# A y step's exp(cum) computed on ScalarE from the row tile already loaded, with that row loaded three slots ahead

## The chip, the cores and the metric

One core of a Trainium2 chip runs the whole kernel as one launch. The metric is the device time of that launch in microseconds (us), median over runs. Engines are named as the profile names them: PE is TensorE's matmuls, PEld its weight loads, DVE is VectorE, ACT is ScalarE, POOL is GpSimd, SP is SyncE, which issues most of the DMAs. POOL issues DMAs too, in its own instruction order.

## What is computed

The reference is one layer of a hybrid sequence mixer: an adaLN-modulated input, one input projection, two branches (a gated linear recurrence A and a Mamba-2 style scan B, both in two directions), gates, and an output projection with a layer norm. The change lies in branch B. Cut to what matters:

```python
cum = jnp.cumsum((dt * a_neg)..., axis=2)            # within a chunk of 128 tokens
y_inter = jnp.einsum('bktgn,bktgr,bkgrnp->bktgrp', cc, jnp.exp(cum), s_prev)
cb = jnp.einsum('bktgn,bksgn->bktsg', cc, bc)
lmat = masked_exp(cum[:, :, :, None] - cum[:, :, None, :], causal)
y_intra = jnp.einsum('bktsg,bktsgr,bksgrp->bktgrp', cb, lmat, x_dt)
return (y_inter + y_intra)
```

There are 1024 latent tokens (8 chunks of 128), 16 heads of 64 channels in 4 groups, a state of 128, and two directions. So `exp(cum)` of a chunk is a row per head and direction, wanted on all 128 partitions.

## The kernel before

All projections are three-pass fp32r matmuls in 128-column blocks (`mm3`, lines 178 to 180). Branch A comes first (to about 560 us of the profile), then branch B in four windows, one for each head group g (`b_window`), then the output projections.

`b_scan(g)` (lines 796 to 912) is the hand-written order of a group: masks and transposes, nine state positions (`xw` on POOL at L843, two matmuls into `bu` at L846, two DVE additions into `St`), then the y loop. The y loop has 16 steps (2 head pairs j, 8 chunks t), each handled in four stages that lag behind one another by `LAGS` slots:

- `loads`: POOL issues a DMA that spreads the row `cum` of two heads and two directions (512 numbers) over 128 partitions, tile L, from the DRAM copy `cum_d` (L868).
- `exponents`: POOL issues a second such DMA, tile e, from `ecum_d`, which holds exp(cum) (L868 again); DVE takes the minimum of L with the tokens' own cum (L878); ACT takes four exps of 128x128 in place, each with its bias column (L881).
- `products`: POOL multiplies e by C (L886), DVE multiplies L by the masked C·B (L887).
- `y_matmuls`: PE multiplies x by L and the states by e into the PSUM tile yi (L902); after four chunks DVE adds yi to y (L905).

Tiles L and e come from a pool of 12 buffers (`w2`) that the state stage and the rms stage share. `cum_d` and `ecum_d` are written once, early, by SP (L703), eight copies of each.

Between the yields of `b_scan` a filler puts projection work of the next group and gates onto PE (`Fill.window`): each yield carries a weight (`W_SCAN` 0.45 for a state position, `W_Y` 0.43 for a y slot) times the group's rate `FILL_B`; a unit is 24 matmuls of 512 columns. Their results go through ACT and DVE too (convolution at L746 and L749, SiLU at L761, gates at L611, weight splits at L162 and L163). A scheduler then sets the order within each engine from the code's order and priorities; each engine runs its own order strictly.

Of the kernel before, what the change touches and what calls it, by code (L numbers as in the profile page):

```python
# [8 lines left out]
P = 128  # L9
# [21 lines left out]
GRAIN = 512  # L31
FILL_T, FILL_A = 0.8, 0.8
GA = (2, 0, 0, 6)
FILL_B = (0.74, 0.64, 0.64, 0.8)
OUT1, OUT2 = 8, 3
GATES = (2, 1, 1, 4)
W_0, W_PRE, W_SCAN, W_Y = 2.0, 1.0, 0.45, 0.43
LAGS = (0, 1, 2, 4)
REP = 8
DT_MIN = 2.0 ** -60  # L40
QT = P
NQT = L // QT
# [61 lines left out]
def hybrid(tc, x, c, ctx, c_ctx, w_mod, b_mod, w_in, lb_logits, a_norm_w, conv_w, conv_b, dt_bias,  # L104
# [3 lines left out]
    nc = tc.nc  # L108
    V, S, T, G = nc.vector, nc.scalar, nc.tensor, nc.gpsimd
# [5 lines left out]
    def pool(st, name, bufs=1, **kw):  # L115
        return st.enter_context(tc.tile_pool(name=name, bufs=bufs, **kw))

    with root:
# [3 lines left out]
        dp = pool(root, "dram", space=DRAM)  # L122
# [5 lines left out]
        def sc(name):  # L128
            return ps.tile([P, 512], F32, tag="sc", bufs=5, name=name)
# [25 lines left out]
        gb_d = dp.tile([D, L], F32, name="gb_d")  # L155

        cum_d = dp.tile([REP, NQT, BH, 2, QT], F32, name="cum_d")
        ecum_d = dp.tile([REP, NQT, BH, 2, QT], F32, name="ecum_d")


        def split(raw, hi, lo):
# [64 lines left out]
        WU = tp_.tile([P, 2, NTA, BH], F32, name="WU")  # L226
        DEC = tp_.tile([P, 2, NTA, BH], F32, name="DEC")
# [5 lines left out]
        with ExitStack() as st:  # L233
# [9 lines left out]
            rows = sp.tile([P, P], F32, name="rows")  # L243
# [186 lines left out]
        def gt(tag, bufs, shape, name):  # L430
            return gp.tile([P] + list(shape), F32, tag=tag, bufs=bufs, name=name)
# [184 lines left out]
        def time_steps():  # L616
# [29 lines left out]
            for i in range(NTA):  # L646
                dst = ta[:, i * 64:(i + 1) * 64] if i < NT else tb[:, (i - NT) * 64:(i - NT + 1) * 64]
# [41 lines left out]
            V.tensor_tensor(fl(WU), fl(WU), DTf, ALU.mult)  # L689
            yield 1.0  # L690

            rows_ = gt("S", 1, [2, L], "crow")[:2 * BH]
            crow, erow = rows_[:, 0, :], rows_[:, 1, :]
            for b in range(2):
                tr = sc(f"cr{b}")
                for i in range(4):
                    T.transpose(tr[:2 * BH, i * P:(i + 1) * P],
                                CUr[:, (b * 4 + i) * 2 * BH:(b * 4 + i + 1) * 2 * BH], ident)
                S.copy(crow[:, b * 512:(b + 1) * 512], tr[:2 * BH, :])
                S.activation(erow[:, b * 512:(b + 1) * 512], tr[:2 * BH, :], AF.Exp)  # L700
            for r_ in range(REP):
                for src, dst in ((crow, cum_d), (erow, ecum_d)):
                    nc.sync.dma_start(dst[r_].rearrange("q h d t -> (h d) q t"),  # L703
                                      src.rearrange("h (q t) -> h q t", t=QT))

        fill = Fill()
        ua = [{} for _ in range(AH)]
# [86 lines left out]
        orders = ((8, 9, 0, 1, 2, 3, 4, 5, 6, 7), (9, 8, 7, 6, 5, 4, 3, 2, 1, 0))  # L794

        def b_scan(g, u):
# [5 lines left out]
            for i0, n in ((8, 2), (0, 4), (4, 4)):  # L802
                tx = sc(f"bb{g}_{i0}")
                for i in range(n):
                    src = Bc[:, (i0 + i) * P:(i0 + i + 1) * P] if i0 < NT else u["Bc"][:, i * P:(i + 1) * P]
                    T.transpose(tx[:, i * P:(i + 1) * P], src, ident)
                S.copy(bt[i0 // 4] if i0 < NT else btc, tx[:, :n * P].rearrange("p (a b) -> p a b", a=n))
            b_tok = lambda i: bt[i // 4][:, i % 4, :] if i < NT else btc[:, i - NT, :]

            CB = bt_("CB", 1, [2, L], f"CB{g}")  # L810
            for b in range(2):
                cb = sc(f"cb{g}_{b}")
                for i in range(4):
                    t = (b * 4 + i) * P
# [6 lines left out]
            xt = bt_("xt", 1, [NT, 2 * P], f"xt{g}")  # L821
            xtc = w2([NTC, 2 * P], f"xtc{g}")
            for i0 in (8, 0, 6, 2, 4):
                tx = sc(f"bx{g}_{i0}")
                for i in range(2):
                    for j in range(2):
                        src = xc[:, j, (i0 + i) * P:(i0 + i + 1) * P] if i0 < NT else u["xcc"][:, j, i * P:(i + 1) * P]
# [1 line left out]
                S.copy(xt[:, i0:i0 + 2, :] if i0 < NT else xtc, tx[:].rearrange("p (a b) -> p a b", a=2))  # L829
            yield W_PRE  # L830

            St = bt_("St", 1, [NT, 2, 256], f"St{g}")
            prev = None
            for pos in range(NTA - 1):
                i0, i1 = orders[0][pos], orders[1][pos]
                by_h = lambda t_: sub(t_[:], i0 * BH + HPG * g, [[(NTA + i1 - i0) * BH, 2], [1, HPG], [0, 64]])
                if pos < NTC:
                    xs_ = sub(xtc[:], (i0 - NT) * 256, [[(i1 - i0) * 256, 2], [64, HPG], [1, 64]])
                else:
                    xs_ = sub(xt[:], i0 * 256, [[(i1 - i0) * 256, 2], [64, HPG], [1, 64]])  # L840
                xw = w2([2, 256], f"xw{g}_{pos}")
                xw4 = xw[:].rearrange("p d (a b) -> p d a b", b=64)
                G.tensor_tensor(xw4, xs_, by_h(WU), ALU.mult)  # L843
                ub = sc(f"bu{g}_{pos}")
                for d, i in ((0, i0), (1, i1)):
                    T.matmul(ub[:, d * 256:(d + 1) * 256], b_tok(i), xw[:, d, :], start=True, stop=True)  # L846
                ub3 = ub[:].rearrange("p (d b) -> p d b", d=2)
                if pos == 0:
                    s0 = w2([2, 256], f"s0{g}")
                    prev = s0[:]  # L850
                    S.copy(prev, ub3)
                else:
                    cur = St[:, pos - 1]
                    V.tensor_tensor(cur.rearrange("p d (a b) -> p d a b", b=64),
                                    prev.rearrange("p d (a b) -> p d a b", b=64), by_h(DEC), ALU.mult)
                    V.tensor_tensor(cur, cur, ub3, ALU.add)
                    prev = cur
                yield W_SCAN


            y = xc
            steps = [(j, t) for j in range(2) for t in range(NT)]
            Ls, Cs, yis = {}, {}, {}

            def rows(src_d, name, j, t):
                t_ = w2([2, 2, P], f"{name}{g}_{j}_{t}")
                src = src_d[0, t, HPG * g + 2 * j, 0, 0:1]
                G.dma_start(t_[:].rearrange("p a b c -> p (a b c)"),  # L868
                                  bass.AP(src.tensor, src.offset, [[NQT * BH * 2 * QT, REP], [0, P // REP], [1, 4 * QT]]))
                return t_  # L870

            def loads(j, t):
                Ls[j, t] = rows(cum_d, "L", j, t)

            def exponents(j, t):
                Cs[j, t] = rows(ecum_d, "e", j, t)
                Lm, h0 = Ls[j, t], HPG * g + 2 * j
                V.tensor_tensor(Lm, Lm, sub(CU[:], t * BH + h0, [[1, 2], [NT * BH, 2], [0, P]]), ALU.min)  # L878
                for h in range(2):
                    for d in range(2):  # L880
                        S.activation(Lm[:, h, d, :], Lm[:, h, d, :], AF.Exp, bias=BIA[:, d, t, h0 + h:h0 + h + 1])  # L881
# [22 lines left out]
                    bs = slice((t - 3) * P, (t + 1) * P)  # L904
                    V.scalar_tensor_tensor(y[:, j, bs], xc[:, j, bs], bd_col(2 * g + j), yi, ALU.mult, ALU.add)  # L905

            for k in range(len(steps) + LAGS[-1]):
                for lag, stage in zip(LAGS, (loads, exponents, products, y_matmuls)):
                    if 0 <= k - lag < len(steps):
                        stage(*steps[k - lag])  # L910
                yield W_Y
# [4 lines left out]
        def z_proj(g, u):  # L916
            for j in range(2):
                blk = 2 * g + j
                for t0, n, acc in (proj_k if blk == 2 * BG - 1 else proj)(O_Z + blk * P, parts_l, f"z{blk}"):
                    if acc is None:  # L920
                        yield n / GRAIN / 4
                        continue
                    with ahead():
                        zs = bt_("gb", 4, [512], f"z{blk}_{t0}")
                        S.activation(zs, acc, AF.Silu)  # L925
                    if g + 1 < BG:
                        z_mul(u, j, t0, zs)
                    else:
                        z_last.append((u, j, t0, zs))
                    yield n / GRAIN / 4  # L930
# [58 lines left out]
        for g in range(BG):  # L989
# [9 lines left out]
            else:  # L999
                fill.add(z_proj(g, ub_[g]), f"z{g}")  # L1000
            fill.window(b_window(g), FILL_B[g])
            fill.until(f"b{g + 1}")
        g = BG - 1
# [129 lines left out]
```

## Time and profile before

| | us |
|---|---|
| median of 3 runs | 1306.72 (1305.6 to 1309.83) |
| the profiled execution | 1304.58 |
| its span | 1302.8 |
| PE busy | 1241.5 (95%) |
| DVE busy | 752.9 (58%) |
| ACT busy | 533.9 (41%) |
| POOL busy | 236.8 (18%) |

Busy shares are means over stages of different kinds. PE's ends are modelled, so a busy PE is not always a PE at its peak. Rows of a group name a line, an engine, the output and inputs, the count, busy time and mean, and then the idle time of that engine just before, with what ended it. The y loops lie at about 583 to 657, 728 to 797, 863 to 933 and 986 to 1062 us.

### The profile page before, as it was taken

What the parts mean: (1) busy time and instruction counts of PE and PEld (TensorE: products, weight loads), DVE (VectorE), ACT (ScalarE), POOL (GpSimd) and SP (SyncE); (2) the same over time, 40 slices, a digit from 0 to 9 for tenths busy, and PEclk for the clock granted to TensorE, in tenths of its full rate; (3) what the DMA queues carried; (4) which work ended last, traced back from release to release, by engine and by line L of the source; (5) the groups of instructions that cost most, each with busy time, mean ns of one, the idle gap of its engine ahead of it and who ended that gap; (6) DMA issues with size and microseconds to landing.
All of it is one profiled execution on the core that took longest, in us unless ns stands there. A gap on an engine that the chain in (4) does not pass through costs nothing.

```text
span 1302.8 us, 18836 instructions
## 1 busy us (share of the span) xinstructions
PE 1241.5 (95%) x7624; PEld 1004.4 (77%) x7624; DVE 752.9 (58%) x988; ACT 533.9 (41%) x851; POOL 236.8 (18%) x264
## 2 busy tenths in 40 slices
PE   5999999999999999999899979998899989999997
PEld 2778888888888888887688757876687668888886
DVE  2426745733836624667575577657646445575568
ACT  2436343432343333337442745364638453213110
POOL 1220000000000000044610662156226520000000
PEclk8999999999999999999999989999899989999999
DMA  9511312112112223125611663156416635662412
GB/s 317 182 40 49 82 33 92 42 35 65 33 33 70 71 75 97 33 65 151 152 39 49 156 147 71 33 147 162 136 58 164 171 98 193 225 248 95 156 41 97
DMA packets 126838, 137.02 MB, mean 105 GB/s; under 512 B 15568, under 2 KB 102288, under 8 KB 126752
## 3 DMA queue, kind: packets, MB, share of 16 engines
q1 hardware_dynamic: 107744, 102.09, 24.8%
q0 software_dynamic: 18656, 33.69, 10.8%
q8 instruction: 60, 0.98, 0.3%
q14 instruction: 26, 0.21, 0.1%
q10 hardware_dynamic: 352, 0.05, 0.0%
HBM read 115.55 MB, written 20.19 MB: 104 GB/s over the span
## 4 chain that ended last, share of the span: by engine, by line
PE 69%; issue 14%; POOL 7%; DVE 4%; DMA 3%; ACT 2%; SPq 0%; POOLq 0%; DVEq 0%; ACTq 0%
PE x L178 4%; PE x L179 3%; PE x L180 3%; POOL e L886 3%; PE f L180 3%; PE f L178 3%; PE f L179 2%; PE ga L178 2%; PE pl L520 2%; PE fo L179 2%; PE fo L180 2%; PE fo L178 2%; PE ga L180 2%; PE ga L179 2%; PE pb L178 2%
## 5 line engine op out<-in xcount | busy, mean ns | idle before, releaser
L881 ACT ACTIVATE L<-L,BIA 128x128 f32<-128x128 f32 x256 | 81.6, 391 | 88.0 <-DVE L L878 87.7
L886 POOL TENSOR_TENSOR e<-e,C 128x512 f32<-128x512 f32 x64 | 92.7, 1448 | 107.5 <-DMA e<-ecum_d 100.6
L843 POOL TENSOR_TENSOR xw<-xtc,WU 128x512 f32<-128x512 f32 x8 | 8.2, 1043 | 566.0 <-ACT xtc L829 566.0
L878 DVE TENSOR_TENSOR L<-L,CU 128x512 f32<-128x512 f32 x64 | 51.1, 800 | 70.4 <-DMA L<-cum_d 51.7
L902 PE MATMUL yi<-L,xt 128*64 128x128 f32 x512 | 44.3, 296 | 28.5 <-DVE L L887 21.8
L887 DVE TENSOR_TENSOR L<-L,CB 128x512 f32<-128x512 f32 x64 | 66.3, 1051 | 6.0 <-ACT L L881 5.9
L902 PEld LDWEIGHTS yi<-L,xt 128*64 128x64 f32 x512 | 28.2, 142 | 51.6 <-DVE L L887 28.3
L749 DVE SCALAR_TENSOR_TENSOR xc<-x,par,xc 128x496 f32<-128x496 f32 (+1 forms) x64 | 47.1, 735 | 13.8 <-ACT xc L746 12.7
L512 ACT COPY KX<-K 128x1024 f32<-128x1024 f32 x28 | 32.1, 1145 | 50.2 <-DVE K L531 45.1
L562 DVE SCALAR_TENSOR_TENSOR S<-S,T,ub 128x128 f32<-128x128 f32 x64 | 22.3, 348 | 51.3 <-ACT S L558 27.6
L178 PE MATMUL fo<-wo,mh 128*128 128x512 f32 x128 | 50.2, 392 | 0.0
L180 PE MATMUL fo<-wo,mh 128*128 128x512 f32 x128 | 49.8, 389 | 0.0
L179 PE MATMUL fo<-wo,ml 128*128 128x512 f32 x128 | 49.8, 389 | 0.0
L531 DVE TENSOR_TENSOR K<-K,T 128x1280 f32<-128x1280 f32 x28 | 46.4, 1658 | 3.4 <-ACT KX L512 1.6
L902 PE MATMUL yi<-e,St 128*64 128x128 f32 x512 | 41.7, 286 | 2.9 <-POOL e L886 2.9
L868 POOL DMA_DIRECT2D L<-cum_d x64 | 39.7, 620 | 0.8 <-DVE L L878 0.7
L533 DVE TENSOR_TENSOR Q<-Q,T 128x1024 f32<-128x1024 f32 x28 | 37.7, 1346 | 3.0 <-PE pl L520 3.0
L868 POOL DMA_DIRECT2D e<-ecum_d x64 | 39.1, 611 | 0.5 <-PE gb L180 0.5
L936 DVE TENSOR_TENSOR xc<-xc,z 128x512 f32<-128x512 f32 x16 | 11.6, 723 | 47.5 <-ACT z L925 47.5
L520 PEld LDWEIGHTS pl<-Q,KX 128*64 128x64 f32 x896 | 30.1, 138 | 9.4 <-issue 8.3
L902 PEld LDWEIGHTS yi<-e,St 128*64 128x64 f32 x512 | 32.3, 145 | 3.8 <-POOL e L886 3.6
L520 PE MATMUL pl<-Q,KX 128*64 128x64 f32 x896 | 34.1, 230 | 0.7 <-DVE Q L533 0.7
(996 smaller groups left out, 3738.9 us busy)
## 6 DMA issues: line engine op xcount, KB each, us to landing
L<-cum_d POOLq DMA_DIRECT2D x64, 256.0 KB, 5.2
e<-ecum_d POOLq DMA_DIRECT2D x64, 256.0 KB, 5.1
wm<-in_w_mod_dram SPq DMA_DIRECT2D x16, 512.0 KB, 7.9
xt<-in_x_dram SPq DMA_DIRECT2D x8, 512.0 KB, 8.4
ga_d<-ga SPq DMA_DIRECT2D x16, 256.0 KB, 2.0
gb_d<-gb SPq DMA_DIRECT2D x16, 256.0 KB, 2.4
m<-ga_d SPq DMA_DIRECT2D x8, 512.0 KB, 4.4
gbt<-gb_d SPq DMA_DIRECT2D x8, 512.0 KB, 7.2
```

Of the source, the lines that this page charges most:

```text
L178: T.matmul(dst, ah, bh, start=(first and i == 0), stop=False)
L179: T.matmul(dst, al, bh, start=False, stop=False)
L180: T.matmul(dst, ah, bl, start=False, stop=(last and i == n - 1))
L520: T.matmul(pl[rows_, t * HP:(t + 1) * HP], KX[:, o:o + HP], qx, start=True, stop=True)
L531: V.tensor_tensor(kv, kv, sub(Ta, lv, [[w, NA // w], [NA - lv, 2], [0, lv]]), ALU.mult)
L749: V.scalar_tensor_tensor(d3[:, :, a:z], r3[:, :, a + o:z + o], cw_col(t, blk), d3[:, :, a:z], ALU.mult, ALU.add)
L868: G.dma_start(t_[:].rearrange("p a b c -> p (a b c)"), bass.AP(src.tensor, src.offset, [[NQT * BH * 2 * QT, REP], [0, P // REP], [1, 4 * Q ...
L878: V.tensor_tensor(Lm, Lm, sub(CU[:], t * BH + h0, [[1, 2], [NT * BH, 2], [0, P]]), ALU.min)
L881: S.activation(Lm[:, h, d, :], Lm[:, h, d, :], AF.Exp, bias=BIA[:, d, t, h0 + h:h0 + h + 1])
L886: G.tensor_tensor(C4, C4, Cc[:, ts].unsqueeze(1).broadcast_to([P, 4, P]), ALU.mult)
L887: V.tensor_tensor(Lm, Lm, CB[:, :, ts].unsqueeze(1).broadcast_to([P, 2, 2, P]), ALU.mult)
L902: T.matmul(yi[h * 64:(h + 1) * 64, o], a, r, start=(k == 0), stop=(k == 3))
```

## The change

exp(cum) of a step is no longer loaded: ACT computes it from tile L (a 128x512 exp into e) before DVE's minimum overwrites L. `ecum_d`, its eight stores and its 64 loads are gone. `LAGS` becomes (0, 3, 4, 5): L is loaded three slots before its exponents, products come one slot after those, the matmuls one slot after the products. The first three loads are issued at state positions 3, 5 and 7 (`EARLY`), so the y loop starts at slot 3 and has 18 slots instead of 20. `FILL_B` is raised. The helper functions of the y loop are moved above the state loop, unchanged but for what is shown.

```diff
-FILL_B = (0.74, 0.64, 0.64, 0.8)
+FILL_B = (0.79, 0.68, 0.68, 0.85)
-LAGS = (0, 1, 2, 4)
+LAGS = (0, 3, 4, 5)
+EARLY = (3, 5, 7)
...
-        ecum_d = dp.tile([REP, NQT, BH, 2, QT], F32, name="ecum_d")
...
-                S.activation(erow[:, b * 512:(b + 1) * 512], tr[:2 * BH, :], AF.Exp)
             for r_ in range(REP):
-                for src, dst in ((crow, cum_d), (erow, ecum_d)):
-                    nc.sync.dma_start(dst[r_].rearrange("q h d t -> (h d) q t"),
-                                      src.rearrange("h (q t) -> h q t", t=QT))
+                nc.sync.dma_start(cum_d[r_].rearrange("q h d t -> (h d) q t"),
+                                  crow.rearrange("h (q t) -> h q t", t=QT))
...
             def exponents(j, t):
-                Cs[j, t] = rows(ecum_d, "e", j, t)
                 Lm, h0 = Ls[j, t], HPG * g + 2 * j
+                Cs[j, t] = w2([2, 2, P], f"e{g}_{j}_{t}")
+                S.activation(Cs[j, t], Lm, AF.Exp)
                 V.tensor_tensor(Lm, Lm, sub(CU[:], t * BH + h0, [[1, 2], [NT * BH, 2], [0, P]]), ALU.min)
...
                     prev = cur
+                if pos in EARLY:
+                    loads(*steps[EARLY.index(pos)])
                 yield W_SCAN
...
-            for k in range(len(steps) + LAGS[-1]):
+            for k in range(len(EARLY), len(steps) + LAGS[-1]):
```

What the scheduler makes of it is shown at two places, both in group 1 at the start of its y loop. In the changed kernel the loads are line 837, the new exp 847, the minimum 848, the four exps 851, the product on POOL 856, on DVE 857, and the y matmuls 872. A name such as L_0_3_5895 is tile L of head pair 0, chunk 3.

POOL in the kernel before, from the last state position on:

```order
L843 TENSOR_TENSOR xw_8_5832<-xt_5454,WU 128x512
L868 DMA L_0_0_5845<-cum_d 128x1x512
L868 DMA L_0_1_5853<-cum_d 128x1x512
L868 DMA e_0_0_5855<-ecum_d 128x1x512
L868 DMA L_0_2_5871<-cum_d 128x1x512
L868 DMA e_0_1_5873<-ecum_d 128x1x512
L868 DMA L_0_3_5895<-cum_d 128x1x512
L886 TENSOR_TENSOR e_0_0_5855<-e_0_0_5855,C_4625 128x512
L868 DMA e_0_2_5897<-ecum_d 128x1x512
L886 TENSOR_TENSOR e_0_1_5873<-e_0_1_5873,C_4625 128x512
```

Here each product stands behind its own load of e and the loads of the next steps.

POOL in the changed kernel at the same place:

```order
L837 DMA L_0_2_5812<-cum_d 128x1x512
L889 TENSOR_TENSOR xw_8_5827<-xt_5450,WU 128x512
L837 DMA L_0_3_5840<-cum_d 128x1x512
L856 TENSOR_TENSOR e_0_0_5842<-e_0_0_5842,C_4614 128x512
L837 DMA L_0_4_5864<-cum_d 128x1x512
L856 TENSOR_TENSOR e_0_1_5866<-e_0_1_5866,C_4614 128x512
L837 DMA L_0_5_5888<-cum_d 128x1x512
L837 DMA L_0_6_5914<-cum_d 128x1x512
L856 TENSOR_TENSOR e_0_2_5890<-e_0_2_5890,C_4614 128x512
L837 DMA L_0_7_5939<-cum_d 128x1x512
```

The loads of chunks 0 to 2 now stand among the state positions, the loads of e are gone, and the load of chunk 7 stands behind the product of chunk 2.

ACT in the kernel before, in the middle of the same y loop (L746 is the filler's convolution):

```order
L881 ACTIVATE L_0_4_5918<-L_0_4_5918,BIA 128x128 x4
L881 ACTIVATE L_0_5_5951<-L_0_5_5951,BIA 128x128
L746 ACTIVATE xc_5944<-x_0_5888,par 128x512
L881 ACTIVATE L_0_5_5951<-L_0_5_5951,BIA 128x128 x3
L881 ACTIVATE L_0_6_5977<-L_0_6_5977,BIA 128x128 x4
L881 ACTIVATE L_0_7_6002<-L_0_7_6002,BIA 128x128 x4
```

Only the four exps of each step stand here, one step after the other.

ACT in the changed kernel at the same place (the convolution is L743 here):

```order
L847 ACTIVATE e_0_4_5941<-L_0_4_5864 128x512
L847 ACTIVATE e_0_5_5973<-L_0_5_5888 128x512
L847 ACTIVATE e_0_6_6006<-L_0_6_5914 128x512
L851 ACTIVATE L_0_4_5864<-L_0_4_5864,BIA 128x128
L743 ACTIVATE xc_5964<-x_0_5881,par 128x512
L851 ACTIVATE L_0_4_5864<-L_0_4_5864,BIA 128x128 x3
L851 ACTIVATE L_0_5_5888<-L_0_5_5888,BIA 128x128 x4
L851 ACTIVATE L_0_6_5914<-L_0_6_5914,BIA 128x128 x4
L847 ACTIVATE e_0_7_6032<-L_0_7_5939 128x512
L847 ACTIVATE e_1_0_6062<-L_1_0_5971 128x512
L851 ACTIVATE L_0_7_5939<-L_0_7_5939,BIA 128x128 x4
```

The new 128x512 exps stand one to three steps ahead of the four small exps of the same step.

## Rows read from the trace of the kernel before

**Rows 1.** Busy time by y loop: PE, PEld, DVE, ACT, POOL; granted clock; DMA

```profile
583.00:657.00 74.00, 70.11 (x487) 54.01 (x486) 48.98 (x67) 45.08 (x89) 38.29 (x44) 1.00 0.56 145
728.00:797.00 69.00, 57.88 (x422) 44.52 (x422) 54.60 (x65) 40.14 (x86) 40.29 (x45) 0.93 0.67 160
863.00:933.00 70.00, 59.44 (x427) 45.74 (x427) 51.15 (x66) 41.17 (x87) 40.62 (x45) 0.93 0.63 165
986.00:1062.00 76.00, 67.91 (x447) 50.92 (x445) 44.37 (x51) 48.21 (x93) 38.98 (x44) 0.93 0.62 161
```

**Rows 2.** The same view of three 5 us windows: full rate, a stall, after it

```profile
865.00:870.00 5.00, 5.00 (x24) 4.16 (x23) 4.83 (x8) 3.62 (x6) 1.62 (x1) 1.00 1.05 215
750.00:755.00 5.00, 1.01 (x10) 1.01 (x12) 4.00 (x6) 3.11 (x9) 3.33 (x4) 0.63 0.41 109
755.00:760.00 5.00, 5.00 (x34) 3.69 (x31) 4.96 (x7) 1.05 (x4) 2.64 (x4) 0.69 0.99 212
```

**Rows 3.** PE's y matmuls of group 1: durations, first and last start

```profile
L902 PE MATMUL yi<-L,xt x128: 272/273/476, 740.9 to 796.8; 128*64 128x128 f32 x128
L902 PE MATMUL yi<-e,St x128: 272/273/421, 741.4 to 797.2; 128*64 128x128 f32 x128
```

**Rows 4.** The chain that ended last: start, length, what (one y step)

```profile
605.14 1.02 PE yi L902 x16
```

**Rows 5.** Who waited for whom, whole execution: total, times, longest

```profile
POOL e L886 <- DMA e<-ecum_d: 100.6, 47, 4.2
ACT L L881 <- DVE L L878: 87.7, 39, 5.3
DVE L L878 <- DMA L<-cum_d: 51.7, 26, 3.9
PEld yi L902 <- DVE L L887: 28.3, 16, 5.3
PE yi L902 <- DVE L L887: 21.8, 10, 4.9
```

**Rows 6.** DMA issues: count, KB each, median us from issue to landing

```profile
L<-cum_d POOLq DMA_DIRECT2D x64, 256.0 KB, 5.2
e<-ecum_d POOLq DMA_DIRECT2D x64, 256.0 KB, 5.1
```

**Rows 7.** Timelines of POOL, DVE and ACT in group 1 (idle before, in brackets)

```profile
745.71 0.62 POOL L868 DMA_DIRECT2D L<-cum_d  x1
750.03 1.59 POOL L886 TENSOR_TENSOR e<-e,C 128x512 f32<-128x512 f32 x1 [3.70 <-DMA e<-ecum_d]
...
752.19 0.59 POOL L868 DMA_DIRECT2D L<-cum_d  x1
...
755.85 1.27 POOL L886 TENSOR_TENSOR e<-e,C 128x512 f32<-128x512 f32 x1 [2.48 <-DMA e<-ecum_d]
...
751.50 0.69 DVE L878 TENSOR_TENSOR L<-L,CU 128x512 f32<-128x512 f32 x1 [1.00 <-DMA L<-cum_d]
...
755.88 1.79 DVE L887 TENSOR_TENSOR L<-L,CB 128x512 f32<-128x512 f32 x1
...
741.26 1.28 ACT L611 ACT_TABLE_LOAD   x1
742.56 0.60 ACT L611 ACTIVATE gb<-gb 128x512 f32<-128x512 f32 x1
```

**Rows 8.** Groups in the whole execution: busy, mean ns, idle before and releaser

```profile
L881 ACT ACTIVATE L<-L,BIA 128x128 f32<-128x128 f32 x256 | 81.6, 391 | 88.0 <-DVE L L878 87.7
L886 POOL TENSOR_TENSOR e<-e,C 128x512 f32<-128x512 f32 x64 | 92.7, 1448 | 107.5 <-DMA e<-ecum_d 100.6
L878 DVE TENSOR_TENSOR L<-L,CU 128x512 f32<-128x512 f32 x64 | 51.1, 800 | 70.4 <-DMA L<-cum_d 51.7
L887 DVE TENSOR_TENSOR L<-L,CB 128x512 f32<-128x512 f32 x64 | 66.3, 1051 | 6.0 <-ACT L L881 5.9
```

**Rows 9.** ACT's groups inside 728 to 797 us

```profile
L881 ACT ACTIVATE L<-L,BIA 128x128 f32<-128x128 f32 x64 | 20.4, 391 | 23.9 <-DVE L L878 23.9
```

**Rows 10.** ACT's only 128x512 exps, in the rms stage, and table loads

```profile
L954 ACT ACTIVATE sq<-sq x6: 630/632/634, 725.4 to 986.7; 128x512 f32<-128x512 f32 x6
L954 ACT ACT_TABLE_LOAD  x6: 1283/1283/1283, 724.1 to 985.4; - x6
```

**Rows 11.** The fastest runs of L878 and L887: minimum, median, maximum ns

```profile
L878 DVE TENSOR_TENSOR L<-L,CU x64: 676/693/1789, 583.9 to 1049.8; 128x512 f32<-128x512 f32 x64
L887 DVE TENSOR_TENSOR L<-L,CB x64: 674/686/2571, 594.2 to 1052.7; 128x512 f32<-128x512 f32 x64
```

More of the change, by code (lines that the diff above doesn't have):

```diff
@@ L690, in time_steps @@
             yield 1.0
-            rows_ = gt("S", 1, [2, L], "crow")[:2 * BH]
-            crow, erow = rows_[:, 0, :], rows_[:, 1, :]
+            crow = gt("S", 1, [2, L], "crow")[:2 * BH, 0, :]
             for b in range(2):
@@ L830, in b_scan, with rows @@
             yield W_PRE
+            y = xc
+            steps = [(j, t) for j in range(2) for t in range(NT)]
+            Ls, Cs, yis = {}, {}, {}
+            def rows(name, j, t):
+                t_ = w2([2, 2, P], f"{name}{g}_{j}_{t}")
+                src = cum_d[0, t, HPG * g + 2 * j, 0, 0:1]
+                G.dma_start(t_[:].rearrange("p a b c -> p (a b c)"),
+                                  bass.AP(src.tensor, src.offset, [[NQT * BH * 2 * QT, REP], [0, P // REP], [1, 4 * QT]]))
+                return t_
@@ new lines, in loads, with exponents @@
+            def loads(j, t):
+                Ls[j, t] = rows("L", j, t)
+            def exponents(j, t):
+                Lm, h0 = Ls[j, t], HPG * g + 2 * j
+                Cs[j, t] = w2([2, 2, P], f"e{g}_{j}_{t}")
+                S.activation(Cs[j, t], Lm, AF.Exp)
+                V.tensor_tensor(Lm, Lm, sub(CU[:], t * BH + h0, [[1, 2], [NT * BH, 2], [0, P]]), ALU.min)
+                for h in range(2):
+                    for d in range(2):
+                        S.activation(Lm[:, h, d, :], Lm[:, h, d, :], AF.Exp, bias=BIA[:, d, t, h0 + h:h0 + h + 1])
@@ new lines, in products, with y_matmuls @@
+            def products(j, t):
+                Lm, Ce, ts = Ls[j, t], Cs[j, t], slice(t * P, (t + 1) * P)
+                C4 = Ce[:].rearrange("p h d t -> p (h d) t")
+                G.tensor_tensor(C4, C4, Cc[:, ts].unsqueeze(1).broadcast_to([P, 4, P]), ALU.mult)
+                V.tensor_tensor(Lm, Lm, CB[:, :, ts].unsqueeze(1).broadcast_to([P, 2, 2, P]), ALU.mult)
+            def y_matmuls(j, t):
+                Lm, Ce = Ls.pop((j, t)), Cs.pop((j, t))
+                if t % 4 == 0:
+                    yis[j] = sc(f"yi{g}_{j}_{t // 4}")
+                yi = yis[j]
+                o = slice((t % 4) * P, (t % 4 + 1) * P)
+                for k in range(4):
+                    for h in range(2):
+                        hs = slice((2 * j + h) * 64, (2 * j + h + 1) * 64)
+                        if k < 2:
+                            a, r = xt[:, t, hs], Lm[:, h, k, :]
+                        else:
+                            a, r = St[:, t if k == 2 else NT - 1 - t, k - 2, hs], Ce[:, h, k - 2, :]
+                        T.matmul(yi[h * 64:(h + 1) * 64, o], a, r, start=(k == 0), stop=(k == 3))
+                if t % 4 == 3:
+                    bs = slice((t - 3) * P, (t + 1) * P)
+                    V.scalar_tensor_tensor(y[:, j, bs], xc[:, j, bs], bd_col(2 * g + j), yi, ALU.mult, ALU.add)
@@ L857, in b_scan @@
                     prev = cur
+                if pos in EARLY:
+                    loads(*steps[EARLY.index(pos)])
                 yield W_SCAN
[L861 to L870, printed above, removed]
@@ L872, in loads @@
-            def loads(j, t):
-                Ls[j, t] = rows(cum_d, "L", j, t)
-            def exponents(j, t):
-                Cs[j, t] = rows(ecum_d, "e", j, t)
[L877 to L881, printed above, removed]
@@ L883, in products @@
-            def products(j, t):
-                Lm, Ce, ts = Ls[j, t], Cs[j, t], slice(t * P, (t + 1) * P)
-                C4 = Ce[:].rearrange("p h d t -> p (h d) t")
-                G.tensor_tensor(C4, C4, Cc[:, ts].unsqueeze(1).broadcast_to([P, 4, P]), ALU.mult)
-                V.tensor_tensor(Lm, Lm, CB[:, :, ts].unsqueeze(1).broadcast_to([P, 2, 2, P]), ALU.mult)
-            def y_matmuls(j, t):
-                Lm, Ce = Ls.pop((j, t)), Cs.pop((j, t))
-                if t % 4 == 0:
-                    yis[j] = sc(f"yi{g}_{j}_{t // 4}")
-                yi = yis[j]
-                o = slice((t % 4) * P, (t % 4 + 1) * P)
-                for k in range(4):
-                    for h in range(2):
-                        hs = slice((2 * j + h) * 64, (2 * j + h + 1) * 64)
-                        if k < 2:
-                            a, r = xt[:, t, hs], Lm[:, h, k, :]
-                        else:
-                            a, r = St[:, t if k == 2 else NT - 1 - t, k - 2, hs], Ce[:, h, k - 2, :]
-                        T.matmul(yi[h * 64:(h + 1) * 64, o], a, r, start=(k == 0), stop=(k == 3))
-                if t % 4 == 3:
-                    bs = slice((t - 3) * P, (t + 1) * P)
-                    V.scalar_tensor_tensor(y[:, j, bs], xc[:, j, bs], bd_col(2 * g + j), yi, ALU.mult, ALU.add)
```

## The prediction

> **What bounds the kernel now.** I read the busy shares first: PE 95%, so only a stage where PE waits can give time back. The view by y loop [rows 1] shows that stage: in the loops of groups 1 to 3 PE is busy 58 of 69, 59 of 70 and 68 of 76 us, and its granted clock is 0.93 there. One 5 us window holds 1.01 us of PE work, and in it and the next the mean granted clock is 0.63 and 0.69, so part of them ran at 1.2 instead of 2.4 GHz [rows 2]. How much is there to win? At full rate PE does 24 filler matmuls in 5 us [rows 2], 0.208 us each, and a y step takes 1.02 us [rows 4]. Between the first and the last y step of group 1 the order of before has filler worth 96 matmuls: 96 x 0.208 + 16 x 1.02 = 36.3 us of work in the 56.3 us from 740.9 to 797.2 [rows 3]. So some 20 us of that loop are waiting or a slow clock. The starts and ends of the loops [rows 1] and the same count give about 10, 20, 20 and 19 us, 69 in all: the most that any change to the y loops alone can return.
>
> What does PE wait for? For DVE's product L887 [rows 5]. Behind that stand ACT waiting for DVE's minimum (87.7 us), DVE waiting for the load of L (51.7) and POOL waiting for the load of e (100.6) [rows 5]. The load lands 5.2 us after its issue [rows 6] and is issued one slot before its use. POOL makes it worse: its product stands in front of later loads and waits for its own e. In the timeline [rows 7] POOL issues a load of L at 745.71, sits 3.70 us until e lands, multiplies, and issues the next load of L only at 752.19; DVE idles 1.00 us for a load before its minimum at 751.50. So the chain is load, POOL, load: two transfers a step behind one in-order engine.
>
> **The change, part by part.** *Loads of e removed.* 64 POOL issues of about 0.6 us go (the issues of L at 752.19 take as long [rows 7]), and with them POOL's 100.6 us of waiting [rows 5]. POOL is left with 1.45 us of product [rows 8] and one issue per step, about 2.05 us, well under a step. The eight stores of ecum_d and two exps at the start of the kernel go too; they lie beside matmuls, so I cost them at nothing; if uncovered, two exps are worth about 1.3 us, by [rows 10].
>
> *Loads of L three slots ahead.* A slot lasts 56.3/16 = 3.5 us now [rows 3] and would be near 3 after, so three slots are 9 us against 0.6 + 5.2 us of issue and landing. The three early loads add 3 x 0.6 us to POOL among the state positions, where POOL does one multiplication in each slot; hidden. The wait of DVE for the load (51.7 us [rows 5]) should go.
>
> *The new exp.* ACT gets 64 exps of 128x512. The rms stage has the same shape and function: 0.632 us [rows 10]. That is 16 x 0.632 = 10.1 us per group, 40 us in all, on an engine that is not yet the bound. The order of the changed kernel has four table loads more in the whole kernel, and the counts in its y loops put them in groups 0 and 3: 2 x 1.283 = 2.6 us each [rows 10]. In the trace a table load costs its 1.28 us and no more: it starts at 741.26 and the next ACT instruction at 742.56 [rows 7].
>
> The Trainium skill, page "ScalarE: Activation LUTs", section "What ACT_TABLE_LOAD costs", speaks against the change: it gives about 1.28 us for the load and 1.38 us more for a drain at each switch of sets. The trace agrees with the first and shows no drain; with it the four loads would cost 10.6 us instead of 5.1, and the predicted time would be some 5 us higher.
>
> *A hop more.* DVE's minimum writes over L, so it now waits for ACT's new exp, and ACT's four exps wait for the minimum. What stands behind a late minimum on DVE are products that PE wants; behind late exps on ACT stand the filler's evacuations. In the order of the changed kernel none of the 64 groups of small exps follows its own large exp directly; up to three large exps run ahead. So I cover this hop with the large exps of other steps; without that cover it costs ACT at least DVE's 0.80 us [rows 8] a step.
>
> *What is late next.* With POOL and the loads gone, ACT is the fullest engine of the y loops. Its busy time by loop is 45.1, 40.1, 41.2 and 48.2 us [rows 1]; with 10.1 more in each and 2.6 in groups 0 and 3 it is 57.8, 50.2, 51.3 and 60.9. To that comes what ACT still waits. In group 1 it idles 69 - 40.1 = 28.9 us now, 23.9 of them for the minimum [rows 9]; 5.0 are for other things and stay. How much hand-off waiting comes back is nowhere in this trace. Its bounds are below nothing (large exps pulled forward fill the 5.0 as well: 3 us of idle time in all) and 10 us on top of the 5 (40% of today's 23.9). I take 4, nearer the low end, since the loads, whose landing is what made the minimum late, are ahead by the longest margin. So 9 us a loop.
>
> The loops then last 57.8 + 9 = 66.8, 59.2, 60.3 and 69.9 us instead of 74, 69, 70 and 76: 7.2 + 9.8 + 9.7 + 6.1 = 32.8 us less. PE allows it: it needs about 10, 20, 20 and 19 us less than today's loops take. DVE allows it barely: 54.6 us of 59.2 in group 1 [rows 1].
>
> *Filler rates.* Two slots fewer at a higher rate: counted in the two orders from the last state matmul to the last y step, PE's work is 49.3, 44.3, 44.3 and 51.2 us before and 46.8, 45.5, 45.5 and 49.3 after. 2.0 us of work leave the loops and have to be done elsewhere on a PE that is full there: plus 2.0.
>
> **The sum.** 1304.58 - 32.8 + 2.0 = 1273.8 us for an execution like the profiled one, which stands 2.1 us under the median of 1306.72; as a median 1275.9, so 1276.
>
> **The rivals.**
> *A. DVE becomes the bound.* L887 lasts 1.05 us in the mean and L878 0.80 [rows 8], but their medians are 0.686 and 0.693 [rows 11]. In the timeline a product on DVE that starts at 755.88 lasts 1.79 us; POOL's product started at 755.85 and lasted 1.27 [rows 7]: DVE waited it out and then did its 0.6. Excess now: 64 x (1.051 - 0.686) + 64 x (0.800 - 0.693) = 30 us, 7.5 a group. If in tighter loops every product of POOL (16 x 1.45 = 23 us a group) falls on a DVE instruction, DVE has 15 us more per group: 64, 70, 66 and 59. Group 1 then gains nothing and group 2 some 4 us; groups 0 and 3 keep their 7 and 6 or so. 17 less 2 is 15 us: 1292. Against it: DVE is not always in an instruction of this kind.
>
> The Trainium skill, page "SBUF — State Buffer", section "Who interferes with whom", says that a DVE instruction with two SBUF inputs contends with a GpSimd instruction that reads SBUF and that the loser blocks fully. The trace agrees (1.79 us against 0.69), and the rule makes this rival as strong as it is.
>
> *B. No change, because the loads are not early after all.* POOL runs in order: the load of chunk 7 stands behind the product of chunk 2, which waits for ACT's exp. If ACT falls behind, loads are issued late again and ACT waits for them: with 17 us of ACT idling a group instead of 9, the loops last 74.8, 67.2, 68.3 and 77.9, 0.8 less than now in sum, and with the 2.0 of filler: 1308. It decides from a load issued less than 5.8 us before its exp. Against it: in the order shown, ACT has over ten instructions between the two.
>
> *C. Slower: the hop is not covered.* Place: ACT, between a large exp and the four small ones. If ACT has to sit through DVE's minimum and what DVE has queued ahead of it (a product, 1.05 us, and a convolution of about 0.7), it idles 2.6 us a step; on half of the steps that is 21 us a group, loops of 57.8 + 5 + 21 = 83.8, 76.2, 77.3 and 86.9, which is 35 us more than now: 1344. It makes the kernel slower from about 13 us of new idling a group, 0.8 us a step, in group 1 (69 - 50.2 - 5). For it: that is only DVE's minimum itself. Against: the large exps run ahead.
>
> *D. The cover is complete.* ACT waits only 3 us a loop: 24 us more than forecast, 1252, PE then having little left to wait for.
>
> **How the numbers follow.** Forecast 1276: 0.60, with 5 to 13 us of ACT waiting a loop (1260 to 1292). A: 0.13, around 1292. B: 0.08, 1308. C: 0.07, anything above 1311. D: 0.12, 1252 and somewhat under. The range takes the forecast, D to its price and A: 1252 to 1298. Outside it lie B, C and the far side of D, about 0.2. A measurement of this kernel can tell about 0.3% (4 us) from no change. Faster by more: 0.60 + 0.13 + 0.12 = 0.85; within: 0.08; slower: 0.07.
>
> **What would show it.** Right: PE's y matmuls of group 1 take about 47 us from first to last instead of 56; POOL's wait for a DMA before its product is gone and it waits for ACT instead; DVE's wait for the load of L is near nothing; ACT is above 80% busy in the y loops; the granted clock there is nearer to 1. Wrong: DVE is busy to the last tenth with L857 above 1.3 us (A); DVE or ACT wait for the load again (B); ACT's small exps wait more than 20 us a group for the minimum (C).

## The result, and the profile after

The changed kernel took 1292.7 us against 1306.2, ratio 0.988 [0.983, 0.992]. One of its four executions, the one that was profiled, took 2451.9 us for a reason that stays open, and the ratio leaves it out. Measured again (run `e1_after`, from which the rows below come) it took 1290.8 us against 1309.6: 0.986 [0.984, 0.989]. By the ratios that is 16 to 18 us faster. The forecast was 1276 (some 31 us faster), the range 1252 to 1298.

> The changed kernel once more, for an ordinary profile and a narrower interval. Known so far: about 1292 us against 1306. The forecast's own account (ACT waits 9 us a y loop, loops of 67, 59, 60 and 70 us) gave 1276, so some 16 us are missing. Theory A (DVE, held up by POOL's product): L857 and L848 on DVE above 1.3 and 0.9 us in the mean, DVE over 90% busy in the loops of groups 1 and 2. Theory C (the hop ACT to DVE to ACT is not covered): ACT idles more than 13 us a loop before its small exps, waiting for the minimum L848. Theory B (loads late): DVE or ACT wait for the load of L. Time 1287 to 1294.

Where did the gain come from? The view of the y matmuls, one line per group of heads, first and last start:

```profile
L872 PE MATMUL yi<-e,St x128: 272/273/273, 604.1 to 655.0; 128*64 128x128 f32 x128
L872 PE MATMUL yi<-e,St x128: 272/273/421, 737.3 to 792.5; 128*64 128x128 f32 x128
L872 PE MATMUL yi<-e,St x128: 272/273/421, 867.9 to 921.6; 128*64 128x128 f32 x128
L872 PE MATMUL yi<-e,St x128: 272/273/421, 986.0 to 1045.6; 128*64 128x128 f32 x128
```

In the kernel before the last step of each group started at 656.5, 797.2 [rows 3], 933.1 and 1061.8. So the changed kernel is ahead by 1.5, 4.7, 11.5 and 16.2 us after the four groups: 1.5, 3.2, 6.8 and 4.7 per group, where the forecast had 7.2, 9.8, 9.7 and 6.1. All of the gain is in branch B: the whole span is 15.4 us shorter.

Busy time by y loop (columns as in [rows 1]):

```profile
583.00:656.00 73.00, 70.18 (x483) 54.28 (x482) 60.81 (x70) 57.07 (x109) 29.29 (x28) 0.98 0.31 90
727.00:793.00 66.00, 59.02 (x439) 46.38 (x438) 58.10 (x68) 50.38 (x103) 29.47 (x28) 0.95 0.31 94
858.00:922.00 64.00, 58.12 (x436) 45.49 (x435) 58.76 (x68) 50.32 (x104) 29.53 (x28) 0.95 0.33 104
977.00:1046.00 69.00, 61.51 (x427) 46.35 (x426) 48.91 (x48) 55.09 (x106) 26.94 (x26) 0.95 0.31 100
```

ACT is 12.0, 10.2, 9.2 and 6.9 us fuller per loop, near the 10 to 13 that were expected but for the last. But DVE is fuller too: 60.8, 58.1, 58.8 and 48.9 us against 49.0, 54.6, 51.2 and 44.4, although nobody gave it work. The groups say which instruction (columns as in [rows 8], and for the last two lines as in [rows 11]):

```profile
L848 DVE TENSOR_TENSOR L<-L,CU 128x512 f32<-128x512 f32 x64 | 98.7, 1569 | 0.8 <-ACT e L847 0.8
L856 POOL TENSOR_TENSOR e<-e,C 128x512 f32<-128x512 f32 x64 | 89.7, 1408 | 110.8 <-ACT e L847 107.2 <-DVE xc L746 3.2
L851 ACT ACTIVATE L<-L,BIA 128x128 f32<-128x128 f32 x256 | 81.1, 390 | 37.7 <-DVE L L848 37.3
L857 DVE TENSOR_TENSOR L<-L,CB 128x512 f32<-128x512 f32 x64 | 47.9, 751 | 22.1 <-ACT L L851 21.6
L848 DVE TENSOR_TENSOR L<-L,CU x64: 677/1770/3859, 585.1 to 1035.6; 128x512 f32<-128x512 f32 x64
L856 POOL TENSOR_TENSOR e<-e,C x64: 1263/1292/1815, 584.9 to 1035.1; 128x512 f32<-128x512 f32 x64
```

The waits of branch B, columns as in [rows 5]:

```profile
POOL e L856 <- ACT e L847: 107.2, 32, 6.7
ACT L L851 <- DVE L L848: 37.3, 27, 3.4
PEld yi L872 <- DVE L L857: 24.4, 15, 4.4
DVE L L857 <- ACT L L851: 21.6, 25, 2.8
PE yi L872 <- DVE L L857: 18.1, 7, 4.0
```

No wait for a load is left among them: the 100.6 and 51.7 us of [rows 5] are gone. In their place DVE's minimum L848 has doubled, from a mean of 0.80 to 1.57 us, with a median of 1.77 where it was 0.693 [rows 11]; L857 has become shorter (0.75 for 1.05). The timeline of group 1 shows why (POOL, DVE, ACT):

```profile
746.39 1.26 POOL L856 TENSOR_TENSOR e<-e,C 128x512 f32<-128x512 f32 x1 [5.47 <-ACT e L847]
748.26 1.29 POOL L856 TENSOR_TENSOR e<-e,C 128x512 f32<-128x512 f32 x1
...
750.12 1.30 POOL L856 TENSOR_TENSOR e<-e,C 128x512 f32<-128x512 f32 x1
...
761.27 1.29 POOL L856 TENSOR_TENSOR e<-e,C 128x512 f32<-128x512 f32 x1 [1.40 <-ACT e L847]
...
746.42 6.16 DVE L848 TENSOR_TENSOR L<-L,CU 128x512 f32<-128x512 f32 x3
...
761.30 1.80 DVE L848 TENSOR_TENSOR L<-L,CU 128x512 f32<-128x512 f32 x1
...
760.57 0.61 ACT L847 ACTIVATE e<-L 128x512 f32<-128x512 f32 x1
```

The large exp ends at 761.18. It releases two instructions at once: POOL's product, which reads e, and DVE's minimum, which overwrites L. They start at 761.27 and 761.30, the minimum is held until the product is through, and takes 1.80 us. This holding of one by the other is called the lock below. Of the three minima that take 6.16 us in a row, the first is held by one product, the second by the two at 748.26 and 750.12 (it takes 3.85 us), the third by none. Counted over the trace, 28 of the 64 minima start within 0.15 us of a product and 46 take more than 0.9 us. Before, minimum and product were released by two different transfers: 3 started so close, and 12 took more than 0.9 us.

### The profile page after: what moved, and what is told of

Its sections match the earlier page's. It is cut to its first block, busy times and chain, and to the rows that moved or that the text cites. A ratio compares the mean times of both kernels' runs of the same rounds, so it can differ in the third digit from the quotient of the medians.

```text
span 2450.1 us, 18712 instructions
## 1 busy us (share of the span) xinstructions
PE 2428.0 (99%) x7624; PEld 1629.8 (67%) x7624; DVE 769.9 (31%) x988; ACT 576.5 (24%) x917; POOL 196.9 (8%) x200
## 4 chain that ended last, share of the span: by engine, by line
PE 99%; DMA 0%; DVE 0%; ACT 0%; SPq 0%; issue 0%; DVEq 0%; ACTq 0%
PE x L178 6%; PE x L179 6%; PE x L180 6%; PE yi L872 5%; PE f L178 3%; PE f L180 3%; PE f L179 3%; PE bu L892 3%; PE gb L178 3%; PE ga L178 2%; PE z L178 2%; PE gb L179 2%; PE ga L180 2%; PE pb L179 2%; PE z L179 2%; PE fo L179 2%
## 5 line engine op out<-in xcount | busy, mean ns | idle before, releaser
L178 PE MATMUL fo<-wo,mh 128*128 128x512 f32 x128 | 87.2, 682 | 0.0
L179 PE MATMUL fo<-wo,ml 128*128 128x512 f32 x128 | 86.4, 675 | 0.0
L180 PE MATMUL fo<-wo,mh 128*128 128x512 f32 x128 | 86.3, 674 | 0.0
L848 DVE TENSOR_TENSOR L<-L,CU 128x512 f32<-128x512 f32 x64 | 65.3, 1033 | 56.3 <-ACT e L847 46.0
L746 DVE SCALAR_TENSOR_TENSOR xc<-x,par,xc 128x496 f32<-128x496 f32 (+1 forms) x64 | 47.0, 735 | 88.7 <-ACT xc L743 87.9
L872 PE MATMUL yi<-e,St 128*64 128x128 f32 x512 | 74.8, 462 | 0.0
L857 DVE TENSOR_TENSOR L<-L,CB 128x512 f32<-128x512 f32 x64 | 61.8, 972 | 30.2 <-ACT L L851 30.2
L872 PE MATMUL yi<-L,xt 128*64 128x128 f32 x512 | 69.9, 423 | 0.0
L847 ACT ACTIVATE e<-L 128x512 f32<-128x512 f32 x64 | 39.4, 625 | 117.7 <-PE yi L872 87.9
L520 PEld LDWEIGHTS pl<-Q,KX 128*64 128x64 f32 x896 | 52.2, 226 | 17.6 <-issue 16.9
L892 PE MATMUL bu<-xw,bt 128*128 128x256 f32 x112 | 58.0, 679 | 0.0
L520 PE MATMUL pl<-Q,KX 128*64 128x64 f32 x896 | 56.4, 319 | 0.0
L179 PEld LDWEIGHTS fo<-wo,ml 128*128 128x128 f32 x128 | 38.4, 300 | 22.1 <-issue 20.6
L178 PEld LDWEIGHTS fo<-wo,mh 128*128 128x128 f32 x128 | 37.9, 296 | 22.2 <-issue 20.1
```

What stands on the lines that cost most here:

```text
L178: T.matmul(dst, ah, bh, start=(first and i == 0), stop=False)
L179: T.matmul(dst, al, bh, start=False, stop=False)
L180: T.matmul(dst, ah, bl, start=False, stop=(last and i == n - 1))
L520: T.matmul(pl[rows_, t * HP:(t + 1) * HP], KX[:, o:o + HP], qx, start=True, stop=True)
L746: V.scalar_tensor_tensor(d3[:, :, a:z], r3[:, :, a + o:z + o], cw_col(t, blk), d3[:, :, a:z], ALU.mult, ALU.add)
L857: V.tensor_tensor(Lm, Lm, CB[:, :, ts].unsqueeze(1).broadcast_to([P, 2, 2, P]), ALU.mult)
```

## The experiments

| run | edit to | us | ratio to before |
|---|---|---|---|
| e1_after | the changed kernel | 1290.8 | 0.986 [0.984, 0.989] |
| e2_exp_only | changed, old lags and rates | 1288.9 | 0.984 [0.982, 0.987] |
| e3_loads_only | before, L three slots ahead, new rates | 1308.8 | 1.000 [0.998, 1.002] |
| e4_no_hop | changed, minimum in its own tile | 1272.2 | 0.972 [0.970, 0.975] |
| e5_product_dve | changed, product of e on DVE | 1255.6 | 0.959 [0.956, 0.962] |
| e6_no_product | changed, product of e left out | 1257.3 | 0.960 [0.958, 0.962] |
| e7_no_hop_old_lags | e4, old lags and rates | 1270.6 | 0.970 [0.968, 0.973] |
| e8_no_hop_product_dve | e4 and e5 together | 1256.9 | 0.960 [0.957, 0.962] |
| e9_both_loads_early | before, L and e two slots ahead, new rates | 1333.7 | 1.018 [1.014, 1.021] |
| e10_before_product_dve | before, product of e on DVE | 1258.3 | 0.960 [0.957, 0.963] |
| e11_product_dve_old_lags | e5, old lags and rates | 1257.4 | 0.959 [0.956, 0.962] |
| e12_product_dve_old_fill | e5, old rates alone | 1256.8 | 0.958 [0.956, 0.961] |

**The two halves of the change.** `e2_exp_only` keeps the exp on ACT and goes back in lags and rates:

```diff
-FILL_B = (0.79, 0.68, 0.68, 0.85)
+FILL_B = (0.74, 0.64, 0.64, 0.8)
-LAGS = (0, 3, 4, 5)
-EARLY = (3, 5, 7)
+LAGS = (0, 1, 2, 4)
+EARLY = ()
```

> Half of the change: the exp on ACT, with the lags (0, 1, 2, 4), no early loads and the filler rates of before. If the gain comes from taking the second load and its wait off POOL, this keeps most of it: 1290 to 1297. If it comes from the three slots of lead, L's load of 5.2 us stays exposed and the hop is added to the chain: 1305 to 1315. My expectation is in between, nearer the second: 1302.

1288.9 us: the exp in place of the second load is the whole gain, against my expectation of 1302. `e3_loads_only` is the kernel before with the early loads of L and the rates of the change, e still loaded:

```diff
-LAGS = (0, 1, 2, 4)
+LAGS = (0, 2, 3, 4, 5)
+EARLY = (3, 5, 7)
...
+            def eloads(j, t):
+                Cs[j, t] = rows(ecum_d, "e", j, t)
```

> The other half: the row L loaded three slots ahead and e still loaded, one slot ahead, POOL with two issues a step, lags (0, 2, 3, 4, 5) for load of L, load of e, exponents, products, matmuls, first three loads among the states, filler rates of the changed kernel. ACT has 40 us less to do than in the changed kernel. If ACT's extra work or its hop holds the changed kernel back (C), this one is faster than it: 1275 to 1285. If DVE with POOL's product holds it (A), it is the same as it or a little slower through POOL's extra issues: 1290 to 1298. If POOL's wait for e holds it, near before: 1300 to 1306.

1308.8 us, ratio 1.000: the lead alone is worth nothing here. Its waits:

```profile
POOL e L860 <- DMA e<-ecum_d: 114.7, 47, 6.1
DVE L L852 <- DMA L<-cum_d: 71.3, 35, 5.4
PE yi L876 <- POOL e L860: 24.5, 14, 4.0
```

POOL waits for e longer than before, and DVE waits for L longer too (71.3 against 51.7 us), though the code loads L three slots ahead. In POOL's order here a load of L isn't issued early, because POOL stands waiting for another load in front of it.

**The hop.** `e4_no_hop` gives the minimum a tile of its own, so that ACT's large exp and DVE's minimum both only read L:

```diff
-                V.tensor_tensor(Lm, Lm, sub(CU[:], ...), ALU.min)
+                M = w2([2, 2, P], f"m{g}_{j}_{t}")
+                V.tensor_tensor(M, Lm, sub(CU[:], ...), ALU.min)
+                Lm = Ls[j, t] = M
```

> The changed kernel with DVE's minimum written into a tile of its own, so that it no longer waits for ACT's large exp; the work of all engines is the same, the tile pool has one tile more alive. Theory C: 10 us or more faster than the changed kernel (1275 to 1283). Theory A: no change, within 4 us (1288 to 1296).

1272.2 us, 18.7 less than the changed kernel. The median of the minimum is back at 0.684, though its mean is not:

```profile
L849 DVE TENSOR_TENSOR m<-L,CU x64: 673/684/2082, 591.7 to 1021.4; 128x512 f32<-128x512 f32 x64
L849 DVE TENSOR_TENSOR m<-L,CU 128x512 f32<-128x512 f32 x64 | 67.7, 1059 | 0.9 <-PE yi L874 0.9
L859 DVE TENSOR_TENSOR m<-m,CB 128x512 f32<-128x512 f32 x64 | 67.8, 1059 | 15.2 <-ACT m L853 15.1
```

So the hop is what stood between forecast and result. But as a serial step, or as what brings POOL and DVE together?

**The lock.** `e5_product_dve` keeps the hop and takes POOL out:

```diff
-                G.tensor_tensor(C4, C4, Cc[:, ts].unsqueeze(1).broadcast_to([P, 4, P]), ALU.mult)
+                V.tensor_tensor(C4, C4, Cc[:, ts].unsqueeze(1).broadcast_to([P, 4, P]), ALU.mult)
```

> The changed kernel with the product of e and C on DVE instead of POOL: POOL then multiplies nothing in the y loops. In the changed kernel's trace DVE's minimum has a median of 1.77 us against 0.69 before, and starts within 0.1 us of POOL's product, both released by the same large exp. Theory K (collision: the large exp releases both at once, and the minimum waits the product out): the minimum falls to 0.69; DVE saves about 64 x 0.9 + 4 and pays 64 x 0.69 for the products, so its load stays, but the chain exp, minimum, exps gets 1.1 us shorter on most steps: 1272 to 1284. Theory H (the hop itself, the mere serial order of ACT and DVE, costs the 19 us): 1288 to 1296.

1255.6 us, faster than either theory said, 35 less than the changed kernel, with one letter changed. The groups of its y loops:

```profile
L857 DVE TENSOR_TENSOR L<-L,CB 128x512 f32<-128x512 f32 x64 | 43.8, 685 | 19.5 <-ACT L L851 19.4
L848 DVE TENSOR_TENSOR L<-L,CU 128x512 f32<-128x512 f32 x64 | 42.8, 684 | 4.7 <-ACT e L847 4.6
L856 DVE TENSOR_TENSOR e<-e,C 128x512 f32<-128x512 f32 x64 | 43.0, 683 | 0.0
L872 PE MATMUL yi<-L,xt 128*64 128x128 f32 x512 | 42.1, 285 | 0.1
```

Three instructions of 0.684 us each, 129.6 us, instead of two that took 146.6: DVE does 64 products more and is busy for less. PE no longer waits before its y matmuls (0.1 us). Theory K, which priced only the minimum's 1.1 us a step, was still 16 us short. `e6_no_product` leaves the product out altogether (the y matmuls read exp(cum) without C):

```diff
-                C4 = Ce[:].rearrange("p h d t -> p (h d) t")
-                G.tensor_tensor(C4, C4, Cc[:, ts].unsqueeze(1).broadcast_to([P, 4, P]), ALU.mult)
```

> The changed kernel without the product of e and C (left out; the y matmuls read exp(cum) itself). Hop and order stay, POOL only issues loads in the y loops, DVE's load falls by what it waited for POOL. K: the minimum falls to 0.69 and the time to that of the kernel without the hop or below it: 1262 to 1274. H: the minimum falls too, but ACT still waits for it on each step: 1283 to 1291.

1257.3 us, no faster than with the product on DVE, below what either theory had: the 43 us of products on DVE are fully covered. `e8_no_hop_product_dve` is e4 with the edit of e5:

> No hop and the product of e and C on DVE: no lock between DVE and POOL in the y loops at all. DVE pays 64 x 0.69 = 44 us and saves 64 x 2 x 0.37 = 47 us of waiting. Rival A (DVE is the bound of what is left): no change against 1272, within 4 us. If POOL's product was off the path and DVE is not the bound: slower by up to 8 us from DVE's longer queue. If the waits on the lock were on the path: 1262 to 1268.

1256.9 us. Without POOL's product the hop costs nothing (1255.6 with it, 1256.9 without); with POOL's product it costs 18.7 us. The serial order alone, theory H, falls; the collision, theory K, stands. Moving the product also takes it out of POOL's queue and makes it shorter, but neither explains the difference: in the changed kernel nothing waits for a load, and PE never waits for POOL's product. What e4 still lost, 15 us against e8, fits the lock met less often: 16 of its minima start within 0.15 us of a product, and its minimum and product on DVE both have a mean of 1.06 us, against 0.684.

**Lead and rates, with nothing else in the way.** `e7_no_hop_old_lags` and `e11_product_dve_old_lags` put the old lags and rates (the diff of e2) into e4 and e5, `e12_product_dve_old_fill` the old rates alone into e5:

> The kernel without the hop (minimum in a tile of its own, 1272 us) with the lags (0, 1, 2, 4), no early loads and the filler rates of before. The exp alone, with the hop, was as fast at the old lags (1289) as the whole change (1291). If that means that the lead of three slots is worth nothing in itself, this is 1270 to 1276. If the lead was worth something but was hidden behind the hop, the load of L is exposed again: 1280 to 1290. I expect the second, at 1281.

> The changed kernel with the product on DVE (1255.6 us), with the lags (0, 1, 2, 4), no early loads and the filler rates of before. If the lead of three slots is worth anything once nothing else holds the loops, this is slower: 1260 to 1270. If not: 1254 to 1258, which is what I expect after the same test with the lock in place gave nothing.

> The changed kernel with the product on DVE and the filler rates of before, lags and early loads as changed: the filler rates alone. With PE no longer waiting in the loops it should not matter where the filler's work lies: 1254 to 1258. Otherwise the loops with less filler show PE waiting again, and the time rises by up to 6 us.

1270.6 against 1272.2, 1257.4 and 1256.8 against 1255.6: in no setting is the lead of three slots, or are the rates, worth anything that can be measured. For e7 I had expected 1281.

**Was it ever the transfer?** `e10_before_product_dve` is the kernel before, both loads and the old lags kept, with the edit of e5 alone:

> The kernel before with one edit: the product of e and C on DVE instead of POOL. Both rows are still loaded, with the lags of before. POOL's queue then only issues loads, which wait for nothing but free buffers; DVE and POOL do not meet in the y loops. If POOL's product (its lock on DVE, and its waiting in front of the next loads) is what held the kernel before, this is near the best kernel without any exp on ACT: 1256 to 1268. If the transfer time of the loads holds it, 1290 to 1305. I expect the first, at 1268, with one slot of lead too short for a landing of 5 us here and there.

1258.3 us, ratio 0.960 [0.957, 0.963]: that one letter, without any part of the change, gives three times what the change gives. And once it is in place the change adds nothing that can be measured (e5 has 0.959 [0.956, 0.962]). The landing times of this run (columns as in [rows 6]):

```profile
L<-cum_d POOLq DMA_DIRECT2D x64, 256.0 KB, 7.3
e<-ecum_d POOLq DMA_DIRECT2D x64, 256.0 KB, 6.7
```

And its waits:

```profile
POOL e L868 <- PE yi L902: 71.2, 33, 7.8
ACT L L881 <- DVE L L878: 45.7, 25, 5.2
DVE e L886 <- DMA e<-ecum_d: 13.1, 10, 3.4
DVE L L878 <- DMA L<-cum_d: 11.3, 15, 1.8
```

The loads take 7.3 us instead of 5.2 [rows 6], and yet less of them is waited for: DVE waits 11.3 us for L, where it was 51.7 [rows 5], and 13.1 for e, where POOL waited 100.6. POOL, which in the y loops now only issues loads, runs ahead until it waits for a buffer that PE gives back (71.2 us). So the kernel before was held by POOL's product: it waited for its own load in front of the next loads in the same queue, and it locked DVE (means of 0.80 and 1.05 us [rows 8], 0.686 and 0.683 here). How much is due to the one and how much to the other, no run separates.

The last run asked the opposite: both loads early, product left on POOL. Like e3 it has the raised rates, and the matmuls one slot behind the products instead of two.

```diff
-LAGS = (0, 1, 2, 4)
+LAGS = (0, 0, 2, 3, 4)
+EARLY = (5, 7)
```

> The loads-only half once more, with both rows, L and e, loaded two slots ahead (lags 0, 0, 2, 3, 4; two first steps among the states), both by DMA, POOL with two issues and the product a step. In the run with only L three slots ahead POOL still waited 115 us for e and nothing was gained. If the exposed transfers are what holds the kernel before, as the forecast had it, this gains most of what the exp on ACT gains: 1285 to 1295. If POOL's product and its lock on DVE are the larger part, it gains little: 1296 to 1308.

1333.7 us, 1.8% slower than before, outside both expectations. Its waits:

```profile
POOL e L860 <- DMA e<-ecum_d: 104.1, 46, 5.8
DVE L L852 <- DMA L<-cum_d: 91.2, 35, 5.1
```

The lag in the code isn't the distance in the queue. POOL's order in this kernel, in group 0:

```
L840 DMA e_0_4_4835<-ecum_d 128x1x512
L840 DMA L_0_5_4862<-cum_d 128x1x512
L840 DMA e_0_5_4864<-ecum_d 128x1x512
L860 TENSOR_TENSOR e_0_4_4835<-e_0_4_4835,C_4185 128x512
L860 TENSOR_TENSOR e_0_5_4864<-e_0_5_4864,C_4185 128x512
L840 DMA L_0_6_4888<-cum_d 128x1x512
```

The scheduler put the product of chunk 5 two places behind the load of its own e, and the loads of chunk 6 behind both. At this place POOL waits 2.65 us before the first product and 0.43 before the second, and issues no load meanwhile. In sum, though, its wait for e is hardly longer than before (104.1 for 100.6 us); what has grown is DVE's wait for L, from 51.7 to 91.2. That this makes the 23 us is read from the order and the waits; no run isolates it, nor the share of the shorter lag of the matmuls.

## Why the prediction was right, and where it was off

The range held the time and the direction was right; the size was 31 us forecast against 16 to 18. That the range reached far enough is owed to rival A; the forecast's own account ended at 1292 with 13 us of ACT waiting a loop, and the waiting was longer.

- **What bounds before.** Right in its chain (load, POOL, load), wrong in its weight: I took the transfer's 5.2 us for the cause and POOL's place in the queue for an aggravation. e10 shows it the other way round: with a longer transfer and POOL's product gone nothing is lost.
- **"Loads of L three slots ahead": the wait of DVE for the load should go.** It went, but by the removal of the second load: in e2, with the old lag, ACT's large exp, which now reads L first, waits 10.1 us for it, of the 51.7 before. The lead was worth nothing in time (e1 against e2, e4 against e7, e5 against e11).
- **The new exp.** 64 exps with a mean of 0.618 us against 0.632 forecast: right. ACT's busy time came out at 57.1, 50.4, 50.3 and 55.1 us against 57.8, 50.2, 51.3 and 60.9, so 7 us less in sum, most of it in group 3.
- **"A hop more", costed at nothing, covered by the large exps of other steps.** This is the step that failed. Large exps of other steps do run ahead, one to three of them on every step; but I followed only ACT's and DVE's order, and not what else the large exp releases. It releases POOL's product too, and the product locks the minimum. Price: 64 x (1.569 - 0.800) = 49 us on DVE, and 18.7 us of time (e1 against e4).
- **ACT's waiting, 9 us a loop.** It was 15.9, 15.6, 13.7 and 13.9 us (loop less busy time): 59 us instead of 36. Those 23 us more, less the 7 us of work that didn't come, put the sum at 1292, the measured time. In group 1 ACT waits 8.9 us for the minimum, where I took 4:

```profile
L851 ACT ACTIVATE L<-L,BIA 128x128 f32<-128x128 f32 x64 | 20.3, 390 | 9.1 <-DVE L L848 8.9
```

- **Filler rates, plus 2.0 us.** The old rates in e5 (e12) changed nothing that can be measured.
- **Rival A** named the mechanism, the lock, and its price of 1292 is the measured time. It had the wrong instruction (L857 above 1.3 us; it was L848) and a chance of 0.13, because I took meetings of DVE and POOL as chance. The change made them the rule. That the price fits is in part luck: A had DVE as the bound, with gains of some 7, 0, 4 and 6 us by group, and they were 1.5, 3.2, 6.8 and 4.7; and e5, which gives DVE 64 instructions more, is faster.
- **The Trainium skill**, page "SBUF — State Buffer", section "Who interferes with whom": the rule that a DVE instruction with two SBUF inputs contends with a GpSimd instruction that reads SBUF agrees with these runs: median 1.77 us for the minimum in e1, 0.683 (0.678 to 0.693 for all 64) in e5, where POOL multiplies nothing in the loops.
- **Rivals B, C and D** didn't come about as priced: no load was late (B), ACT waited 37 us in all for the minimum and not 84 (C), and PE was left waiting 18 us before its y matmuls (D). C had the right place, the hop, but not the reason.
- **The signs that I set.** 47 us from the first to the last y step of group 1: it was 55.7. The loop starts earlier (736.8) and holds more filler (137 other matmuls between the two, for 114); the last steps of the groups are the better measure. ACT was to be over 80% busy in the loops, and was 76 to 80%. The waits for loads went, as set.

## What to carry to other kernels

When a step gets a new producer, list everything that it releases and look in a trace which of those instructions hold one another up: here two that are freed by one event collided on most steps (46 of 64), where freed by different events they had collided now and then (12 of 64). Before moving loads earlier in code, look at what stands in front of them in the queue that issues them; a compute instruction that waits for its own load there undid the lead (e3). The cheapest test of both is to move that one instruction to another engine, even to the busier one: here it was worth 35 to 52 us, and the change itself 16 to 18.

## What the runs showed of the hardware that I had not expected

In these loops DVE does three 128x512 fp32 instructions with two SBUF inputs faster alone (3 x 0.684 us) than two of them beside one of POOL's (1.57 + 0.75 us in the changed kernel). In the changed kernel, wherever the two start within 0.15 us of each other (28 of 64), POOL's product kept its usual 1.3 us and the minimum was the one that was held; in e4 that was so in 11 of 16. POOL's product can be held too: 17 in the changed kernel take 1.5 to 1.8 us, and each of them starts while a DVE instruction of this kind is running. In each group one minimum took 3.83 to 3.86 us, across two of POOL's products with 0.6 us between them; why it doesn't get its turn in that gap is open.

The granted clock in the loops followed the stalls: 0.93 in three loops before, 0.95 in the changed kernel, 1.00 in e4 and e5, where PE hardly pauses. So part of each gain, between the levels of 1.2 and 2.4 GHz, is put down to the clock: for the same 7624 matmuls PE was busy 1241.5 us before, 1236.8 in e1, 1227.2 in e4 and 1225.7 in e5. From e1 to e4 that is 9.6 of the 17.0 us by which the profiled span fell.
